# Layer 0 of a two-layer encoder: two modulation steps moved ahead, and the first gate's transpose put behind the keys' products

## The chip, the core and the metric

The kernel runs on one core of a Trainium2 chip. The metric is the time of one execution in microseconds (us), as the device gives it. Before the change three runs took 2202.97, 2203.79 and 2204.16 us; the median is 2203.79 us. Engines are named as in the profile: PE is TensorE (matrix products and transposes), DVE is VectorE, ACT is ScalarE, POOL is GpSimd, SP is the engine whose queue issues nearly all DMAs.

## What is computed

Two layers on x of 256 tokens by 2048 channels, conditioned on one vector c. The part that matters here:

```
c_act = silu(c)
for l in range(2):
    mod = c_act @ w_mod[l] + b_mod[l]            # 6 vectors of 2048
    shift_m, scale_m, gate_m, shift_f, scale_f, gate_f = split(mod, 6)
    h = layer_norm(x) * (1 + scale_m) + shift_m
    proj = h @ w_in[l]                            # four head groups A, B, C, D
    y = concat(A: gated MLP, B: latent attention, C: short conv, D: conformer conv) @ w_out[l]
    x = layer_norm(ALPHA * x + (1 + gate_m) * y) * g + b
    h = layer_norm(x) * (1 + scale_f) + shift_f
    x = layer_norm(ALPHA * x + (1 + gate_f) * conv_ffn(h)) * g + b
```

Group B squeezes h to latents, normalises them, turns them, and makes from them the rotated keys, the queries (`qn`, `qr`), the keys (`kn`) and the values (`vv`) for a four-head attention.

## The kernel before, in words

**Modulation as background work.** The 12 vectors of `mod` (six for each layer) are made on DVE. One vector is 16 steps; a step (`mod_block`, line 190) loads a block of `w_mod` of 128 x 2048 floats (1 MB) by SP's queue into one of four raw buffers and multiplies it with `crep` on DVE, with the sum over the columns as result (line 196). Layer 0's `SHIFT_M` and `SCALE_M` come first, in the planner of `by_blocks`. All other steps come from a generator, `mods`, in a fixed order that begins with `(0, GATE_M)` and goes on with `(0, SCALE_F)`.

**Pacing.** `stream` (line 337) treats one unit of weights: it loads the unit, records the products of the unit before, and calls `pump` (line 307). `pump` adds the rate of the present phase to a credit and takes one step for each whole credit. The rates stand in `RATES` (line 35); for layer 0 they are 1.3 a unit in phase B, 1.3 at each of four points inside the attention ("attend"), and 1.9 in phase C. Since the rows of a gate are needed across the partitions, `gate_rows` (line 268) turns the finished vector on PE (`turn`), copies it by ACT, writes it to DRAM (`line`) and reads it back to all partitions by SP (`spread`); both are chores that are tried after a step.

**The stretch around the change** (layer 0, some 150 to 330 us). Group B's latents are made from eight units of `w_in` of two pairs of 128 x 704 each (`latent_group`; the loads are named `wexact`), then four values' worth of weights for the attention are loaded (`wq`, `wkv`), then three steps are taken at once (`MODS_AHEAD`), and the latents are turned. Two DVE operations of the turned latents, `kc` and `kvr`, are tied behind the last of these three steps:

```
def behind(i):
    if stepped:
        tc.add_manual_dep(i.ins, stepped[0], order_dep, reason="these steps' weights land before the latents turn")
```

`kc` feeds the rotated key (`ps_kr` on PE). There are two PSUM buffers ("ms") for all these small products, so the first `ps_qn` needs the buffer that the second `kvr` reads. Meanwhile group C's eight units of products (`C_c`, 32 rows of the trace a unit) are recorded between the parts of the attention. DVE and ACT also work off, in the background, the 31 taps of group D's convolution (`convD`, `scaled`), and DVE the norm of group A's half (`va`), which needs a transfer `gmlp` into a raw buffer. Then comes the output projection: two units of plain float32 weights, then units whose weights ACT and DVE split into two parts (`whi` by ACT line 391, `wlo` by DVE line 400), and in between the rest of group D's norm: `ps_var`, `rd`, `dgD`, `ps_rD`.

Instructions are recorded in program order; a scheduler sets the order on each engine, and each engine then runs its list in order.

Of the kernel before, what the change touches and what calls it, by code (L numbers as in the profile page):

```python
# [31 lines left out]
SHIFT_M, SCALE_M, GATE_M, SHIFT_F, SCALE_F, GATE_F = range(6)  # L32


RATES = [
    dict(B=1.3, attend=1.3, C=1.9, out=1.0, out_next=0.0, out_last=0.0, out_tail=0.5, up_first=0.5, up_late=0.75, up_renewed=0.75, up_third=0.6, up=0.75, down=0.7, down_next=0.45, down_last=0.3, down_tail=0.5),
    dict(D=1.0, U=0.0, V=0.0, B=0.0, C=0.0, E=1.35, attend=0.0, out=0.75, out_next=0.6, out_last=0.0, out_tail=0.0, up_first=0.3, up_late=0.3, up_renewed=0.3, up_third=0.3, up=0.3, down=0.7, down_next=0.7, down_last=0.0, down_tail=0.0),
]

# [49 lines left out]
def encoder_kernel(ctx: ExitStack, tc: tile.TileContext, A: dict, consts: bass.AP, out: bass.AP):  # L89
# [22 lines left out]
    def ms_tile(name):  # L112
        return msp.tile([P, 512], F32, tag="ms", name=name)

    def acc_tile(name):
        return accp.tile([P, 512], F32, tag="acc", name=name)

    def mm(o, lhsT, rhs, start, stop):
        return pe.matmul(o, lhsT, rhs, start=start, stop=stop, skip_group_check=True)  # L119
# [4 lines left out]
    def slot(name, dtype=F32):  # L124
        return slotp.tile([P, 1024], dtype, tag="slot", name=name)
# [75 lines left out]

    GATE = {}
    closed = []
    GATES = [(l, m) for l in range(DEPTH) for m in (GATE_M, GATE_F)]

    chores = []
# [61 lines left out]
    def gate_rows(l, m, cols):  # L268

        line = dramp.tile([KT, P], F32, name=f"line_{l}_{m}")  # L270

        def turn():
            if pace["phase"].startswith("up"):
                return False
            ps = ms_tile("ps_gate")
            pe.transpose(ps[0:KT, 0:P], cols, ident)
            rows = keep.tile([KT, P], F32, tag="rows", name=f"rows_{l}_{m}")
            act.copy(rows, ps[0:KT, 0:P])
            nc.scalar.dma_start(out=line, in_=rows)
            return True  # L280

        def spread():
            if GATES.index((l, m)) > len(closed) + 1:
                return False
            if (l, m) == (1, GATE_M) and pace["phase"] in ("down", "down_next", "down_last", "down_tail", *"VDUBC"):
                return False
            g = gatep.tile([P, D], F32, tag="gate", name=f"gate_{l}_{m}")
            i = nc.sync.dma_start(out=g, in_=line.rearrange("k c -> (k c)").partition_broadcast(P))
            if (l, m) == (1, GATE_M):
                tc.add_manual_dep(i.ins, last_issue[0], order_dep, reason="layer 0's transfers come first")  # L290
            GATE[(l, m)] = g
            return True

        return [turn, spread]
# [3 lines left out]
        + [(0, GATE_F, 0, 3), late_steps, (0, GATE_F, 3, KT), (1, SHIFT_M), (1, SCALE_M)]  # L298
        + [(1, GATE_M), (1, SHIFT_F), (1, SCALE_F), (1, GATE_F)]
    )  # L300
    pace = {"rate": 0.0, "credit": 0.0, "phase": None}

    def phase(l, name):
        pace["phase"] = name
        pace["rate"] = RATES[l][name]

    def pump():
        pace["credit"] += pace["rate"]
        while pace["credit"] >= 1.0:
            pace["credit"] -= 1.0  # L310
            next(mods, None)
# [25 lines left out]
    def stream(load, products, bg=0):  # L337

        item = load()
        flush()  # L340
        pending.append(lambda: products(item))
        pump()
        for _ in range(min(bg, len(background))):
            background.pop(0)()
        if late["tasks"]:
            late["tasks"].pop(0)()
# [176 lines left out]
    def latent_group(w, c0, name, then, hF=None, bg=0):  # L523

        nk = 2
        box = {}

        def products(item, u):
            if u == 0:
                box["wide"] = [acc_tile(f"{name}_w{t}")[:, 0:Q_LORA] for t in range(2)]  # L530
                box["narrow"] = [acc_tile(f"{name}_n{t}")[:, 0 : 704 - Q_LORA] for t in range(2)]
                box["h"] = list(hT)
            for k, (hi, lo) in enumerate(item):
                kt = u * nk + k
                st, sp = kt == 0, kt == KT - 1
                for t in range(2):
                    tok = slice(t * P, (t + 1) * P)
                    outs = ((box["wide"][t], slice(0, Q_LORA)), (box["narrow"][t], slice(Q_LORA, 704)))
                    if lo is None:
                        for o, c in outs:  # L540
                            mm(o, hF(kt)[:, tok], hi[:, c], st, sp)
                        continue
                    xh, xl = (h[:, kt % 2, tok] for h in box["h"][kt // 2][:2])
                    for o, c in outs:
                        mm(o, xh, hi[:, c], st, False)
                    for o, c in outs:
                        mm(o, xh, lo[:, c], False, False)
                    for o, c in outs:
                        mm(o, xl, hi[:, c], False, sp)

        def load(u):
            return weights(w, u * nk, nk, c0, 704, hF is not None)

        return KT // nk, load, products, lambda: then(box["wide"], box["narrow"]), bg
# [27 lines left out]
    def run(g, ahead=0):  # L582
        units, load, products, end, bg = g
        loaded = []

        def get(u):
            while len(loaded) < min(u + 1 + (ahead if u > 0 else 0), units):
                loaded.append(load(len(loaded)))
            return loaded[u]

        for u in range(units):
            n = bg[u] if isinstance(bg, tuple) else bg
            stream(lambda: get(u), lambda item, u=u: products(item, u), n)
            pending.extend(postponed)
            postponed.clear()
        pending.append(end)
# [258 lines left out]
    def mixers(l, w_in, Y, hF=None, first_mod=None, quarter=None):  # L855
# [10 lines left out]
        def more_mods():  # L866
            pace["credit"] += RATES[l]["attend"]
            rate, pace["rate"] = pace["rate"], 0.0
            pump()
            pace["rate"] = rate  # L870
# [199 lines left out]
        def mix_b(wide, narrow):  # L1070
# [40 lines left out]


            steps = attend(WQ, WKV, lat, q01, rr)

            def step():
# [7 lines left out]
        def attend(WQ, WKV, lat, q01, rr):  # L1123
# [60 lines left out]
            for b in range(2):  # L1184
                ps = ms_tile("ps_kn")
                for hh in range(2):
                    h = 2 * b + hh
                    for j in range(2):
                        mm(
                            ps[:, hh * S : (hh + 1) * S],  # L1190
                            WKV[j][:, h * S : h * S + P],
                            kvr[:, j, :],
                            j == 0,
                            j == 1,
                        )
                act.copy(kn[:, 2 * b : 2 * b + 2, :], ps.rearrange("p (j s) -> p j s", j=2))
            more_mods()
            vv = slot("vv").rearrange("p (t c) -> p t c", t=2)
            for t in range(2):
# [143 lines left out]
        if hF is not None:  # L1343
            return by_blocks(l, w_in, hF, first_mod, quarter, mix_d, mix_u, gelu_v, mix_v, mix_b, mix_c, mix_e)
# [21 lines left out]
    def by_blocks(l, w_in, hF, first_mod, quarter, mix_d, mix_u, gelu_v, mix_v, mix_b, mix_c, mix_e):  # L1366
# [87 lines left out]
        sumE = total("E")  # L1454
        postponed.append(mix_v)
        phase(l, "B")
        run(latent_group(w_in, C_Q, f"B{l}", mix_b, hF=hf, bg=STEPS[l]["B"]))
        phase(l, "C")

# [329 lines left out]
def build(inputs):  # L1789
    import numpy as np  # L1790
    import concourse.bacc as bacc

    nc = bacc.Bacc("TRN2", target_bir_lowering=False, num_devices=1)
    v = {name: np.asarray(a, dtype=np.float32) for name, a in inputs.items()}
    arrays, A = {}, {}
    direct = {name: v[name] for name in _PLAIN}
    direct.update(params=_params(v), gmlp=_gmlp(v), consts=_constants(), late=_late(v))
    for name, a in direct.items():
        a = np.ascontiguousarray(a)
        arrays[f"in_{name}_dram"] = a  # L1800
        A[name] = nc.dram_tensor(f"in_{name}_dram", a.shape, F32, kind="ExternalInput").ap()
    for name in _PACKED:
        A[name] = Packed(nc, name, v[name].size)
    consts = A["consts"]
    out = nc.dram_tensor("out_0_dram", (1, S, D), F32, kind="ExternalOutput").ap()
    with tile.TileContext(nc) as tc:  # L1806
        encoder_kernel(tc, A, consts, out)
    for name in _PACKED:
        arrays[f"in_{name}_dram"] = A[name].array(v[name])
    return nc, arrays  # L1810
# [8 lines left out]
```

## Time and profile before

| | |
|---|---|
| median of three runs | 2203.79 us (2202.97 to 2204.16) |
| the profiled execution's own time | 2203.58 us |
| its span | 2201.8 us, so 1.8 us lie around it |
| PE busy | 2174.7 us, 99% of the span |
| DVE busy | 1740.8 us, 79% |
| ACT busy | 1101.8 us, 50% |
| DMA | 617.07 MB, mean 280 GB/s |

The profile is one execution. Busy times are sums over an engine's instructions; "idle before" is the time that an engine stood still in front of an instruction, with what ended it behind the arrow. [...]

### The profile page before, as it was taken

Reading aid. Unit: us, or ns where it says so; the run is one execution under the profiler, and the core shown is the slowest. Engines: PE = TensorE matmul, PEld = TensorE weight load, DVE = VectorE, ACT = ScalarE, POOL = GpSimd, SP = SyncE. Lnnn points to the kernel's source line nnn. Section 1 sums busy time; section 2 is a strip of 40 time slices with the busy share of each in tenths; the row PEclk is TensorE's granted clock in tenths of the full one; section 3 lists DMA queues with packets and bytes.
Section 4 is the critical chain, followed back from the end, with each engine's and each line's share of the span. In section 5 each row is a group of like instructions: output and inputs, shape, how many; then the busy total and the mean of one; then the engine's idle time right before and its main releaser. Section 6 shows DMA issues by size and latency. Waiting matters only on the chain. (4 is left out here: it accounts for less than half of the span.)

```text
span 2201.8 us, 28483 instructions
## 1 busy us (share of the span) xinstructions
PE 2174.7 (99%) x10916; PEld 1805.2 (82%) x10916; DVE 1740.8 (79%) x2325; ACT 1101.8 (50%) x1686; POOL 22.1 (1%) x40
## 2 busy tenths in 40 slices
PE   8999999999999999999999999999999999999997
PEld 6776878688888888888868988868888888888886
DVE  5658999789898888889978988977776755565777
ACT  3132744655555455545574545465444544454553
POOL 0000000000000000000000000000000000000000
PEclk9999999999999999999999999999999999999999
DMA  9999888688989988987768547956766655555554
GB/s 392 417 374 390 355 331 334 232 334 319 333 329 334 338 324 328 361 323 285 291 230 323 205 152 292 332 222 244 267 244 244 227 191 189 191 210 192 197 196 141
DMA packets 94906, 617.07 MB, mean 280 GB/s; under 512 B 10737, under 2 KB 10929, under 8 KB 27441
## 3 DMA queue, kind: packets, MB, share of 16 engines
q1 hardware_dynamic: 94466, 614.70, 75.2%
q8 instruction: 85, 1.39, 0.2%
q0 software_dynamic: 176, 0.53, 0.1%
q14 instruction: 51, 0.42, 0.0%
q10 hardware_dynamic: 128, 0.03, 0.0%
HBM read 613.08 MB, written 2.13 MB: 279 GB/s over the span
## 5 line engine op out<-in xcount | busy, mean ns | idle before, releaser
L391 ACT CAST whi<-wraw 128x1024 fp32r<-128x1024 f32 (+1 forms) x620 | 643.9, 1045 | 687.8 <-PE g_c L119 207.2
L400 DVE TENSOR_TENSOR wlo<-wraw,whi 128x1024 fp32r<-128x1024 f32 (+1 forms) x620 | 743.7, 1212 | 287.5 <-ACT whi L391 268.6
L119 PE MATMUL v_c<-hT,whi 128*128 128x512 f32 x1408 | 489.4, 392 | 0.0
L196 DVE SCALAR_TENSOR_TENSOR wmod<-wmod,crep 128x2048 f32<-128x2048 f32 x192 | 438.2, 2285 | 52.4 <-DMA wmod<-in_w_mod_dram 51.7
L119 PE MATMUL g_c<-hT,whi 128*128 128x512 f32 x1280 | 444.7, 392 | 0.0
L119 PE MATMUL v_c<-hT,wlo 128*128 128x256 f32 x1408 | 392.3, 279 | 0.0
L119 PE MATMUL d<-whi,a 128*128 128x512 f32 x1344 | 386.4, 389 | 0.0
L119 PE MATMUL g_c<-hT,wlo 128*128 128x256 f32 x1280 | 356.5, 278 | 0.0
L119 PEld LDWEIGHTS v_c<-hT,whi 128*128 128x128 f32 x1408 | 263.7, 187 | 59.4
L119 PEld LDWEIGHTS d<-whi,a 128*128 128x128 f32 x1344 | 252.0, 188 | 52.5
L119 PEld LDWEIGHTS g_c<-hT,whi 128*128 128x128 f32 x1280 | 239.7, 187 | 54.2
L119 PEld LDWEIGHTS v_c<-hT,wlo 128*128 128x128 f32 x1408 | 265.1, 188 | 0.0
L119 PEld LDWEIGHTS g_c<-hT,wlo 128*128 128x128 f32 x1280 | 241.0, 188 | 0.0
L119 PE MATMUL d<-wlo,a 128*128 128x512 f32 x672 | 232.9, 389 | 0.0
L119 PEld LDWEIGHTS d<-wlo,a 128*128 128x128 f32 x672 | 126.1, 188 | 26.2
L119 PE MATMUL o<-whi,a 128*128 128x512 f32 x416 | 121.4, 393 | 0.0
L119 PEld LDWEIGHTS o<-whi,a 128*128 128x128 f32 x416 | 78.6, 189 | 16.3
L425 DVE TENSOR_TENSOR a<-g,a 128x512 fp32r<-128x512 f32 x132 | 87.5, 682 | 0.0
L569 PE MATMUL first<-wexact,hN 128*128 128x512 f32 x192 | 85.5, 596 | 0.3
L421 ACT CAST a<-g 128x512 fp32r<-128x512 f32 x132 | 77.0, 615 | 0.0
L1535 DVE SCALAR_TENSOR_TENSOR u<-g,par,u 128x254 f32<-128x254 f32 (+1 forms) x176 | 74.3, 478 | 0.2
L119 PE MATMUL o<-wlo,a 128*128 128x512 f32 x208 | 72.8, 394 | 1.2 <-DVE wlo L400 1.2
(316 smaller groups left out, 2151.3 us busy)
## 6 DMA issues: line engine op xcount, KB each, us to landing
wmod<-in_w_mod_dram SPq DMA_DIRECT2D x192, 1024.0 KB, 7.2
wraw<-in_ffn_w_up_dram SPq DMA_DIRECT2D x168, 1024.0 KB, 5.2
wraw<-in_ffn_w_down_dram SPq DMA_DIRECT2D x88, 1024.0 KB, 5.1
wexact<-in_w_in_dram SPq DMA_DIRECT2D x64, 512.0 KB, 11.3
wraw<-in_w_out_dram SPq DMA_DIRECT2D x30, 1024.0 KB, 7.1
wraw<-in_w_in_dram SPq DMA_DIRECT2D x24, 1024.0 KB, 5.6
wexact<-in_ffn_w_up_dram SPq DMA_DIRECT2D x16, 512.0 KB, 5.0
wlate<-in_late_dram SPq DMA_DIRECT2D x8, 1024.0 KB, 6.5
```

The source lines that it names most:

```text
L119: return pe.matmul(o, lhsT, rhs, start=start, stop=stop, skip_group_check=True)
L196: i = dve.scalar_tensor_tensor(out=raw, in0=raw, scalar=1.0, in1=crep, op0=ALU.mult, op1=ALU.mult, accum_out=col)
L391: i = act.copy(hi[:, :m], r)
L400: i = dve.tensor_tensor(out=lo[:, :m], in0=r, in1=hi[:, :m].bitcast(F32), op=ALU.subtract)
L421: i = act.copy(hi, src)
L425: dve.tensor_tensor(out=lo, in0=src, in1=hi.bitcast(F32), op=ALU.subtract)
L569: i = pe.matmul(ps, hN[kt // 4][:, kt % 4, t * P : (t + 1) * P], parts[kt], start=kt == 0, stop=kt == KT - 1, skip_group_check=True,)
L1535: dve.scalar_tensor_tensor(out=u[:, sh:], in0=x[:, : S - sh], scalar=col(k, j), in1=u[:, sh:], op0=ALU.mult, op1=ALU.add)
```

## The change

Three things. In phase C the rate falls from 1.9 to 1.65 a unit. In phase B the first three units each get 0.7 of credit on top of 1.3 (`pace["more"]`); so two steps more are taken in group B's units and two fewer in group C's. And `turn` of `(0, GATE_M)` refuses until `keyed` holds something, which is so once the keys' products (`ps_kn`) have been recorded.

```diff
-    dict(B=1.3, attend=1.3, C=1.9, out=1.0, ...
+    dict(B=1.3, attend=1.3, C=1.65, out=1.0, ...
...
     closed = []
+    keyed = []
...
         def turn():
             if pace["phase"].startswith("up"):
                 return False
+            if (l, m) == (0, GATE_M) and not keyed:
+                return False
             ps = ms_tile("ps_gate")
             pe.transpose(ps[0:KT, 0:P], cols, ident)
...
-    pace = {"rate": 0.0, "credit": 0.0, "phase": None}
+    pace = {"rate": 0.0, "credit": 0.0, "phase": None, "more": []}
...
     def pump():
         pace["credit"] += pace["rate"]
+        if pace["more"]:
+            pace["credit"] += pace["more"].pop(0)
...
                 act.copy(kn[:, 2 * b : 2 * b + 2, :], ps.rearrange("p (j s) -> p j s", j=2))
+            keyed.append(True)
             more_mods()
...
         phase(l, "B")
+        pace["more"] = [0.7, 0.7, 0.7]
         run(latent_group(w_in, C_Q, f"B{l}", mix_b, hF=hf, bg=STEPS[l]["B"]))
```

What this does to the engines' lists shows at three places. In the changed kernel line numbers behind line 204 are up to seven higher.

The first is SP's queue through group B's units. `wexact` 128x704 is a unit's pair of weights, `wmod` a step's block. Before:

```order
L375 DMA wexact<-in_w_in_dram 128x704 x2
L194 DMA wmod<-in_w_mod_dram 128x2048
L375 DMA wexact<-in_w_in_dram 128x704 x2
L1033 DMA gmlp<-in_gmlp_dram 128x2048
L194 DMA wmod<-in_w_mod_dram 128x2048
L375 DMA wexact<-in_w_in_dram 128x704 x2
L194 DMA wmod<-in_w_mod_dram 128x2048
L375 DMA wexact<-in_w_in_dram 128x704 x2
L194 DMA wmod<-in_w_mod_dram 128x2048 x2
```

With the change:

```order
L380 DMA wexact<-in_w_in_dram 128x704 x2
L194 DMA wmod<-in_w_mod_dram 128x2048 x2
L380 DMA wexact<-in_w_in_dram 128x704 x2
L1038 DMA gmlp<-in_gmlp_dram 128x2048
L194 DMA wmod<-in_w_mod_dram 128x2048 x2
L380 DMA wexact<-in_w_in_dram 128x704 x2
L194 DMA wmod<-in_w_mod_dram 128x2048 x2
L380 DMA wexact<-in_w_in_dram 128x704 x2
L194 DMA wmod<-in_w_mod_dram 128x2048
```

Six blocks instead of three stand ahead of the fourth unit's pair, one fewer stands behind it, and ten becomes twelve over the eight units; the three blocks of `MODS_AHEAD` stay where they are, behind `wkv`, and are now the 13th to 15th instead of the 11th to 13th.

The second is DVE from the first steps of `(0, GATE_M)` to the turned latents' `kc`. The rows from the first step on, before:

```order
L196 SCALAR_TENSOR_TENSOR wmod,sums_2_837<-wmod,crep 128x2048
L1038 BN_STATS stA<-va 128x6 x2
L603 BN_AGGR mv_A_867<-stA 128x2
L603 BN_AGGR mv_A_876<-stA 128x2
L605 TENSOR_SCALAR rs_A_869<-mv_A_867 128x1
L605 TENSOR_SCALAR rs_A_878<-mv_A_876 128x1
L1421 TENSOR_TENSOR partE<-E_0_811,partE 128x512
L938 TENSOR_TENSOR convD<-convD,scaled 128x4x255
L1421 TENSOR_TENSOR partE<-E_1_812,partE 128x512
```

With the change:

```order
L196 SCALAR_TENSOR_TENSOR wmod,sums_2_837<-wmod,crep 128x2048
L1043 BN_STATS stA<-va 128x6 x2
L196 SCALAR_TENSOR_TENSOR wmod,sums_2_837<-wmod,crep 128x2048
L1427 TENSOR_TENSOR partE<-E_0_811,partE 128x512
L1427 TENSOR_TENSOR partE<-E_1_812,partE 128x512
L608 BN_AGGR mv_A_870<-stA 128x2
L608 BN_AGGR mv_A_879<-stA 128x2
L943 TENSOR_TENSOR convD<-convD,scaled 128x4x255
L610 TENSOR_SCALAR rs_A_872<-mv_A_870 128x1
L610 TENSOR_SCALAR rs_A_881<-mv_A_879 128x1
```

The second step has moved from behind the four `va` operations to ahead of `partE`; behind the rows shown one more tap (128x4x254), then the four `va` operations and then the third step follow. Later on, eight steps in a row stand ahead of `kc` before, and nine with the change; the third of `MODS_AHEAD` is the last of them in both.

The third is PE at the output projection's first split unit (`o_...`; `ps_var` and `ps_rD` belong to group D's norm). Before:

```order
L119 MATMUL ps_var<-ones,sqD_1680 128x1 x2
L119 MATMUL ps_var<-ones,sqD_1681 128x1 x2
L119 MATMUL o_000_1655<-whi,a 128x512
L119 MATMUL o_001_1656<-whi,a 128x512
L119 MATMUL o_000_1655<-wlo,a 128x512
```

With the change:

```order
L119 MATMUL ps_var<-ones,sqD_1680 128x1 x2
L119 MATMUL ps_var<-ones,sqD_1681 128x1 x2
L119 MATMUL ps_rD<-dgD,ones 128x256
L119 MATMUL o_000_1655<-whi,a 128x512
L119 MATMUL o_001_1656<-whi,a 128x512
L119 MATMUL o_010_1657<-whi,a 128x512
L119 MATMUL o_011_1658<-whi,a 128x512
L119 MATMUL o_000_1655<-wlo,a 128x512
```

`ps_rD` stood 28 products further on and now comes directly behind `ps_var`. Elsewhere on PE, `ps_gate` moves from among group C's products to behind `ps_kn`, the first transpose of the latents moves from ahead of group C's first unit to behind it, and most of group C's second and third unit moves from ahead of `ps_qr` and `ps_kn` to behind the scores.

## Rows read from the trace of the kernel before

**Rows 1.** The page, busy time of PE: us, share of span, instructions.

```profile
PE 2174.7 (99%) x10916; PEld 1805.2 (82%) x10916; DVE 1740.8 (79%) x2325; ACT 1101.8 (50%) x1686; POOL 22.1 (1%) x40
```

**Rows 2.** Waits of PE, first 450 us: us in total, times, longest.

```profile
...
PE ps_qn L119 <- DVE kvr L1151: 1.2, 1, 1.2
PE o L119 <- DVE wlo L400: 1.2, 2, 0.9
PE ps_kr L119 <- DVE kc L1147: 1.2, 1, 1.2
PE o L119 <- DMA wexact<-in_w_out_dram: 1.1, 1, 1.1
...
```

**Rows 3.** Busy time by stretch, last three columns: PE's clock, DMA share, GB/s.

```profile
core 0: us, PE busy (x) PEld busy (x) DVE busy (x) ACT busy (x) POOL busy (x), PEclk, DMA share, GB/s
...
160.00:172.00 12.00, 12.00 (x55) 8.80 (x54) 10.74 (x15) 7.41 (x19) 0.11 (x1) 1.00 0.65 234
172.00:210.00 38.00, 37.04 (x137) 25.23 (x135) 28.41 (x27) 8.04 (x26) 1.63 (x3) 1.00 1.02 416
...
232.00:240.00 8.00, 8.00 (x38) 6.79 (x38) 8.00 (x10) 6.98 (x19) 0.00 (x0) 1.00 0.18 51
240.00:290.00 50.00, 49.90 (x240) 42.24 (x240) 49.73 (x70) 28.07 (x71) 0.00 (x0) 1.00 0.93 370
```

**Rows 4.** Timeline of SP's queue: start us, us, what, how many.

```profile
162.54 6.36 SPq L194 DMA_DIRECT2D wmod<-in_w_mod_dram  x2
168.98 0.86 SPq L375 DMA_DIRECT2D wexact<-in_w_in_dram  x2
```

**Rows 5.** Timeline of DVE: start us, us, what, how many, idle before.

```profile
164.92 1.41 DVE L1043 SCALAR_TENSOR_TENSOR va<-va,rs_A,gmlp 128x512 f32<-128x512 f32 x2
166.25 2.28 DVE L196 SCALAR_TENSOR_TENSOR wmod<-wmod,crep 128x2048 f32<-128x2048 f32 x1
...
207.65 2.29 DVE L196 SCALAR_TENSOR_TENSOR wmod<-wmod,crep 128x2048 f32<-128x2048 f32 x1 [0.19 <-DMA wmod<-in_w_mod_dram]
...
210.13 2.29 DVE L196 SCALAR_TENSOR_TENSOR wmod<-wmod,crep 128x2048 f32<-128x2048 f32 x1 [0.17 <-DMA wmod<-in_w_mod_dram]
...
212.34 0.41 DVE L1146 TENSOR_TENSOR kc<-ps_q,cst 64x256 f32<-64x256 f32 x1
...
215.61 0.47 DVE L1151 TENSOR_SCALAR kvr<-ps_kv,par 128x256 f32<-128x256 f32 x1
```

**Rows 6.** Timeline of PE, the turned latents and what follows.

```profile
202.87 7.07 PE L119 MATMUL C_c<-hF,wexact 128*128 128x256 f32 x32
...
213.23 0.67 PE L119 MATMUL ps_kr<-kc,cst 64*128 64x256 f32 x2 [1.18 <-DVE kc L1147]
...
216.14 8.30 PE L119 MATMUL ps_qn<-qg,wq 128*128 128x256 f32 x24 [1.24 <-DVE kvr L1151]
224.28 11.39 PE L119 MATMUL C_c<-hF,wexact 128*128 128x256 f32 x52
```

**Rows 7.** Busy time by stretch, columns as in rows 3: where the clock was low.

```profile
215.00:222.00 7.00, 5.86 (x14) 4.71 (x15) 4.39 (x6) 3.86 (x10) 0.00 (x0) 0.51 1.04 415
...
314.00:318.00 4.00, 4.00 (x12) 3.10 (x12) 3.12 (x7) 3.27 (x3) 0.70 (x1) 0.57 0.99 412
```

**Rows 8.** Timeline of PE at the output projection's start.

```profile
295.88 14.00 PE L119 MATMUL o<-wexact,ya 128*128 128x512 f32 x32 [1.13 <-DMA wexact<-in_w_out_dram]
309.71 1.84 PE L119 MATMUL ps_var<-ones,sqD 128*128 128x1 f32 x16
...
313.04 0.73 PE L119 MATMUL o<-wlo,a 128*128 128x512 f32 x2 [0.91 <-DVE wlo L400]
```

**Rows 9.** Timeline of DVE, group D's deviation.

```profile
316.24 0.15 DVE L985 TENSOR_SCALAR rd<-ps_var 128x2 f32<-128x2 f32 x1
317.28 0.48 DVE L991 TENSOR_SCALAR dgD<-cst,rd 128x128 f32<-128x128 f32 x2 [0.88 <-POOL rd L149]
```

More of the change, by code (lines that the diff above doesn't have):

```diff
@@ L35 @@
 RATES = [
-    dict(B=1.3, attend=1.3, C=1.9, out=1.0, out_next=0.0, out_last=0.0, out_tail=0.5, up_first=0.5, up_late=0.75, up_renewed=0.75, up_third=0.6, up=0.75, down=0.7, down_next=0.45, down_last=0.3, down_tail=0.5),
+    dict(B=1.3, attend=1.3, C=1.65, out=1.0, out_next=0.0, out_last=0.0, out_tail=0.5, up_first=0.5, up_late=0.75, up_renewed=0.75, up_third=0.6, up=0.75, down=0.7, down_next=0.45, down_last=0.3, down_tail=0.5),
     dict(D=1.0, U=0.0, V=0.0, B=0.0, C=0.0, E=1.35, attend=0.0, out=0.75, out_next=0.6, out_last=0.0, out_tail=0.0, up_first=0.3, up_late=0.3, up_renewed=0.3, up_third=0.3, up=0.3, down=0.7, down_next=0.7, down_last=0.0, down_tail=0.0),
```

## The prediction

> **What bounds the kernel now.** I read the page first: PE is busy for 2174.7 of 2201.8 us [rows 1], so the end moves only by what PE loses or wins: waits, and products at the lower clock. Next the waits of PE in the first 450 us, the only part that the change reorders to any extent: two waits of 1.2 us in the turned latents (for `kc` and for `kvr`), 1.1 us for the first weights of the output projection, and two for `wlo`, 0.9 and 0.3 us [rows 2]. The timeline shows where they lie [rows 6, 8]. The clock's stretches show what comes on top: PE had half of its clock around 215 to 222 us and again around 314 to 318 us [rows 7], each time just behind such waits. The 24 products of `ps_qn` took 8.30 us; at full clock a product of this size takes 0.22 us (32 `C_c` in 7.07 us), which makes 5.3 us, so the first low stretch cost 3.0 us [rows 6]. The second cost about half of 0.43 x 2 x 4.0 us = 1.7 us [rows 7]. All that can be won here is thus near 2.4 + 3.0 + 1.1 + 1.2 + 1.7 = 9.4 us, 0.4% of the time. I count a move under 0.2%, or 4.4 us, as no change, about what a measurement can tell.
>
> **What sets the start of `ps_qn`.** The timeline of DVE answers it: `kc` starts at 212.34, right behind the third of the steps of MODS_AHEAD, and that step (and the one before it) had waited for its block; the two landed 2.48 us apart [rows 5]. So the keys' chain hangs on the 13th block of the first gate, not on DVE. And the queue that brings it was full: from 172 to 210 us the share is 1.02 at 416 GB/s, while from 160 to 172 it was 0.65 [rows 3].
>
> **Part 1, two steps into group B's units.** They put two more blocks of 2.48 us ahead of the block that `kc` hangs on. Used as it is now, the queue brings it 5.0 us later. Could the empty time before 172 us take them in? There are 12 x 0.35 = 4.2 us of it [rows 3], which would leave 0.8 us. But a block needs one of four raw buffers. The second one of the row at 162.54 shows that: its issue took place at 162.54 + 6.36 - 0.33 = 168.57 us, when the second step's product, started at 166.25, had freed a buffer [rows 4, 5]. With the change the sixth block waits in the same way for the third step's product, and that stands behind the `va` operations. These ended at 166.3 us [rows 5]; the new order puts a tap, and four small operations, behind `partE` that were done before it or came later, some 1.2 + 0.6 us, so they end near 168.0, the third product near 170.3, and the sixth block is issued 1.8 us later than the fifth is now. Behind it the fourth unit's pair is still to come (2 x 352 KB, 1.7 us at 416 GB/s), which now goes ahead, and nine blocks instead of eight. By that count the 15th block is 1.8 + 1.7 + 2.5 = 6.0 us late. I take 5.5 us, between 5.0 and 6.0, since both rest on the same full queue; 0.8 stays as the lower bound. The second `kvr` stands one step behind `kc` in both orders, so `ps_qn` starts 5.5 us later. That the first transpose of the latents no longer waits ahead of group C's first unit gives nothing: PE would only wait longer for `kc`. The pairs of group B's units come later too, by a few us; no wait of PE for them stands in rows 2, and a delay of them is covered by the wait for `kc`, which is 7 us or so long now.
>
> **The clock.** In the trace PE was at its lower level for some 5.9 us after `ps_qn` had started (216.14 to 222) and, in the other stretch, for about 4.5 us after the wait that ended at 313.04 [rows 6, 7, 8]. With a longer wait more of the low stretch lies in the wait itself. Ends: nothing at the lower clock (3.0 us won), or all 24 products (10.6 us, 2.3 us lost). I take 1.0 us won, a little beyond what the second stretch's 4.5 us would give (0.7 us). [...] The trace shows the low level behind both gaps (0.51 and 0.57).
>
> **Part 2, two steps fewer in group C, and the gate's transpose.** DVE was busy 49.73 of 50 us from 240 to 290 [rows 3], so two products of 2.29 us fewer let it reach the projection at worst 5.5 - 4.6 = 0.9 us later, while PE comes 5.5 - 1.0 = 4.5 us later. Hence PE's wait of 1.1 us for `wexact` of the output projection goes: its issues follow DVE's steps. The longest waits of PE hold none for group C's products [rows 2]; I cost the new order of group C's products at nothing, since three `C_c` rows of the order, six products or 1.3 us, stand between `ps_qr` and each `ps_qr2` and cover `qc`; without that cover two waits of up to 1.3 us come. The gate's transpose no longer stands among these products; its DMA chain still blocks SP until `line` has landed (share 0.18 from 232 to 240 [rows 3]), now about 3 us later. No wait followed from it before, and the units of group C have been loaded in advance; I cost it at nothing.
>
> **Part 3, `ps_rD`.** It is now directly behind `ps_var`, and must wait for `rd` (0.15), POOL (0.88) and `dgD` (0.48) [rows 9]: 1.6 us with the hops, in which PE does nothing. In turn the wait for `wlo` of 0.9 us is covered, and with it I count the 0.3 us of rows 2: +0.4. The second low stretch I leave as it is, for a wait of this kind stands there again.
>
> **The sum:** + 5.5 - 1.0 - 1.1 + 0.4 = + 3.8 us. The profiled execution took 2203.58 us (2201.8 and 1.8 around it), 0.2 under the median of 2203.79; on that median the forecast is **2207.6 us**, which is 0.17% more, no change by the bound, if close to it.
>
> **Rivals.**
> A, the queue takes the blocks in: the 15th block is 0.8 us late. For it speaks the share of 0.65; against it the buffers. Then 0.8 - 1.0 - 1.1 + 0.4 = - 0.9, and with shorter waits both low stretches may go, 2.0 and 1.7 more: down to - 4.6, 2199.2 us.
> B, slower: the clock stays low through `ps_qn`. Its place is the 24 products behind the long wait, its price 2.3 us lost where I have 1.0 won, so + 7.1, 2210.9 us. It decides if the low stretch still lasts 7 us after `ps_qn` has started; for it speaks that PE will have stood nearly still for longer than in any row, against it that both stretches ended within 5.9 us of PE's restart. [...]
> C, the lateness is made up: DVE, two steps ahead, spares PE every later wait and the 1.6 us too, and the second low stretch goes: 3.8 - 1.6 - 1.7 = + 0.5, about 2204.3 us. That the change does nothing else than it says is not in doubt: the lists of all engines are those of the order.
>
> **How the numbers follow.** Forecast 0.53, with its own range of 2205.5 to 2209.5; of it 0.38 lies within 0.2% and 0.15 beyond. A 0.17, of which 0.10 is faster by over 0.2% and 0.07 within. B 0.20, all slower. C 0.10, within. So faster 0.10, within 0.2% 0.55, slower 0.35. The range leaves out half of A and the upper half of B: 2200 to 2211.5 us. It takes in the bounds of the clock, of the covers (2 x 1.3) and of the queue.
>
> **What would show it.** DVE's `kc` should start near 217.8 instead of 212.34, behind a step that waited for its block; PE's wait for `kc` should be near 7 us; `ps_qn` should start near 221.6 and take 6.5 to 8 us. The wait for `wexact` at the projection should be gone, and a wait of 1.6 us for `dgD` should stand there. If `kc` starts before 214, part 1 is wrong; if `ps_qn` takes 10 us, B is right; if no wait for `dgD` shows, part 3 is.

## The result and the profile after

The changed kernel took 2207.49 us (median of 14 runs, 2205.78 to 2209.94), the kernel before 2202.49 us (14 runs on the same chip, 2201.56 to 2204.62): a ratio of 1.0022, 95% interval 1.0015 to 1.0029. It is slower by some 5 us; that is little, but the two ranges don't overlap. The profiled execution of the change was its shortest (2205.78 us, span 2204.0), that of before (2203.58) was 1.1 us above its median; so the two traces differ by 2.2 us where the medians differ by 5.0. A second trace of the change, from the experiments, shows what the first one hides.

DVE at the turned latents, the rows that answer to those of [rows 5]:

```profile
210.76 2.29 DVE L196 SCALAR_TENSOR_TENSOR wmod<-wmod,crep 128x2048 f32<-128x2048 f32 x1 [8.23 <-DMA wmod<-in_w_mod_dram]
...
215.73 2.29 DVE L196 SCALAR_TENSOR_TENSOR wmod<-wmod,crep 128x2048 f32<-128x2048 f32 x1 [0.18 <-DMA wmod<-in_w_mod_dram]
...
217.95 0.41 DVE L1151 TENSOR_TENSOR kc<-ps_q,cst 64x256 f32<-64x256 f32 x1
...
221.21 0.47 DVE L1156 TENSOR_SCALAR kvr<-ps_kv,par 128x256 f32<-128x256 f32 x1
```

`kc` stands behind the 15th product now, and that one behind its block; it starts at 217.95 instead of 212.34, 5.6 us later. PE's timeline there and at the projection (the counterparts of [rows 6, 8]):

```profile
210.49 0.44 PE L1139 MATMUL ps_kv<-cst,lat 128*128 128x128 f32 x2 [0.23 <-ACT qg L1145]
218.83 1.19 PE L119 MATMUL ps_kr<-kc,cst 64*128 64x256 f32 x2 [7.91 <-DVE kc L1152]
...
221.74 6.70 PE L119 MATMUL ps_qn<-qg,wq 128*128 128x256 f32 x24
...
298.17 13.90 PE L119 MATMUL o<-wexact,ya 128*128 128x512 f32 x32
311.90 1.84 PE L119 MATMUL ps_var<-ones,sqD 128*128 128x1 f32 x16
315.36 0.70 PE L119 MATMUL ps_rD<-dgD,ones 128*128 128x256 f32 x2 [1.62 <-DVE dgD L996]
```

One wait of 7.9 us has taken the place of the two of 1.2; no wait for `wexact` stands at the projection; `ps_rD` waits 1.62 us for `dgD`. Of the waits of PE in the first 450 us (the counterpart of [rows 2]), these three lie in the part that was changed:

```profile
PE ps_kr L119 <- DVE kc L1152: 7.9, 1, 7.9
...
PE ps_rD L119 <- DVE dgD L996: 1.6, 1, 1.6
...
PE o L119 <- DVE wlo L405: 0.2, 1, 0.2
```

The busy time by stretch, with PE's clock, DMA share and GB/s last (the counterpart of [rows 3, 7]; the first two stretches are those of the low clock, 0.50, where the third has the full one, 1.00):

```profile
214.10:224.30 10.20, 5.47 (x12) 3.40 (x13) 9.70 (x13) 2.44 (x7) 0.00 (x0) 0.50 1.01 410
316.50:319.90 3.40, 3.40 (x10) 2.63 (x9) 3.40 (x4) 0.00 (x0) 0.00 (x0) 0.50 0.38 92
160.00:172.00 12.00, 12.00 (x54) 8.83 (x53) 11.09 (x22) 8.80 (x23) 2.55 (x3) 1.00 0.51 193
```

The queue between 160 and 172 us is emptier than before (0.51 against 0.65) although it had more to bring. SP's timeline says why (the counterpart of [rows 4]), with DVE's third step:

```profile
160.37 10.06 SPq L194 DMA_DIRECT2D wmod<-in_w_mod_dram  x2
```

```profile
167.78 2.29 DVE L196 SCALAR_TENSOR_TENSOR wmod<-wmod,crep 128x2048 f32<-128x2048 f32 x1
```

The second of these two issues took place at 160.37 + 10.06 - 0.33 = 170.10 us (0.33 us is what one such issue takes without a wait, as that at 156.86 us): it had to wait for a buffer until the third step's product, which stands behind the `va` operations, had ended at 170.07.

To compare executions whole, I use the lag of PE: the start of one product less the start of group B's first product, against the trace of before (161.92 us there). The points are the starts of the first and the last product of `ps_qn`, of the first of the projection, and of the transposes of layer 0's and layer 1's second norms (before: 216.14, 224.06, 295.88, 391.94 and 1451.64 us). In us, minus is earlier:

| trace | ps_qn first | ps_qn last | projection | norm, layer 0 | norm, layer 1 |
|---|---|---|---|---|---|
| the change | +5.8 | +4.2 | +2.5 | +2.8 | +2.1 |
| the change, second trace | +4.9 | +4.7 | +3.0 | +4.6 | +3.6 |
| e1 kc behind the 13th step | -0.1 | -1.2 | -1.7 | -1.3 | -2.3 |
| e2 before, kc behind the 11th | -0.8 | -3.7 | +3.7 | +6.2 | +5.3 |
| e3 pacing without the gate's delay | +10.5 | +7.5 | +3.4 | +2.2 | +1.3 |
| e4 the gate's delay alone | -0.1 | -0.7 | -0.4 | -1.1 | -1.8 |
| e6 that, and two steps fewer in C | -0.4 | -0.6 | -2.3 | -0.8 | -2.2 |
| e7 kc behind the 11th, gate late | -0.8 | -2.2 | +0.6 | +1.2 | +0.2 |
| e9 the change, rd behind wlo | +4.9 | +4.8 | +3.0 | +2.4 | +1.5 |
| e10 the change, kc freed, gate late | -3.0 | -5.9 | -1.6 | -2.5 | -3.5 |
| e11 kc freed, old pacing, gate late | -1.8 | -4.7 | +5.1 | +3.5 | +3.1 |
| e12 e10 once more | -3.0 | -4.2 | -1.0 | -2.2 | -3.2 |

In some executions, of more than one kernel, the time is longer by several us (e1: 2210.02 and 2211.20 us beside ten runs from 2201.54 to 2204.85), with the products of a long stretch of the FFN 2% slower in the trace of e1; the profiled executions of e8 and e11, 4.7 and 5.7 us above their medians, are taken to be of this kind, so the spans of these three are not used, and their lags only up to that stretch (e8 has no row).

### The profile page after: what moved, and what is told of

Its sections match the earlier page's. It is cut to its first block, busy times and chain, and to the rows that moved or that the text cites. A ratio compares the mean times of both kernels' runs of the same rounds, so it can differ in the third digit from the quotient of the medians.

```text
span 2204.0 us, 28478 instructions
## 1 busy us (share of the span) xinstructions
PE 2173.4 (99%) x10916; PEld 1809.8 (82%) x10916; DVE 1741.5 (79%) x2325; ACT 1100.5 (50%) x1686; POOL 23.3 (1%) x40
```

## The experiments

Each was compared with the kernel before on its own chip. The ratio is to that kernel; its median was 2202.33 us for e1 to e4, 2202.01 for e5 to e8, 2202.03 for e9 and e10, 2204.11 for e11 and e12. The ratio is an estimate with its interval and not the quotient of the two medians; the two differ most where the times scatter (e11: 1.0015 and 1.0026).

### The chain: which block kc hangs on (e1, e2, e3)

**e1**, the change with `kc` and `kvr` tied to the first of the three steps of MODS_AHEAD (the 13th) instead of the third (the 15th):

```diff
                 for _ in range(MODS_AHEAD):
                     next(mods, None)
-                stepped.append(last_step[0])
+                    stepped.append(last_step[0])
```

> The changed kernel, with one edit: kc and kvr are tied behind the first of the three steps of MODS_AHEAD instead of the third; number and places of all steps stay. Theory (the start of ps_qn hangs on the last block that kc is tied to): the 13th block's product ran 210.76 to 213.05 us in the changed kernel, so kc starts near 213.1 instead of 217.95, the second kvr stands behind the 14th product (213.25 to 215.5) and starts near 215.6, ps_qn starts near 216.2 as before the change, PE's wait for kc falls from 7.9 to about 3 us with 1.5 us for kvr, and the time falls by about 4 us to 2203.5 us, the kernel before within 1 us. Rival (kc is late because the latents' transposes moved behind group C's first unit on PE): kc stays behind 216 us, ps_qn near 221, the time stays at 2207.5 us.

Measured: 2202.8 us, ratio 1.0000 (0.9988 to 1.0013). The loss is gone by this one order, within the interval. `kc` started as soon as the 13th product ended:

```profile
209.66 2.29 DVE L196 SCALAR_TENSOR_TENSOR wmod<-wmod,crep 128x2048 f32<-128x2048 f32 x1 [8.24 <-DMA wmod<-in_w_mod_dram]
211.88 0.08 DVE L196 DVE_READ_ACCUMULATOR wmod<-wmod,crep 128x1 f32 x1
211.88 0.41 DVE L1151 TENSOR_TENSOR kc<-ps_q,cst 64x256 f32<-64x256 f32 x1
```

PE waited 2.29 us for it and none for `kvr`, less than was expected, in part since the 13th block had landed 1.1 us earlier than in the change (209.66 against 210.76); `ps_qn` started at 215.67 us. The rival falls: the latents' transposes stand behind group C's first unit here as in the change.

**e2**, the same edit in the kernel before.

> The kernel before, with the same single edit: kc tied behind the 11th step instead of the 13th. In the list of DVE the second kvr now stands behind the 12th product alone. Theory (the block sets kc): the 11th block had landed at 205.07 us, so kc is bound by PE's transposes instead and starts near 211.5; the first kvr follows, then the 12th product of 2.3 us, then the second kvr near 214.5, so ps_qn starts 1.0 us earlier than 216.14; PE's two waits of 1.2 us shrink to about 1.4 in all. Gain 1 us, and up to 4 us if the low stretch of the clock behind them goes too: 2198.5 to 2201.5 us. Rival (DVE and PE, not the block, set kc in the kernel before): kc stays at 212.3, the time within 1 us of the kernel before.

Measured: 2210.75 us, ratio 1.0038 (1.0023 to 1.0052). Neither said this. The chain did what the theory says (`kc` at 211.30, second `kvr` at 214.58, `ps_qn` at 215.10 us, and, with 5.45 us for its 24 products, at full clock), but the win of 3.7 us was lost at once:

```profile
215.10 5.45 PE L119 MATMUL ps_qn<-qg,wq 128*128 128x256 f32 x24 [1.24 <-DVE kvr L1151]
220.39 14.84 PE L119 MATMUL C_c<-hF,wexact 128*128 128x256 f32 x68
239.00 0.27 PE L276 MATMUL ps_gate<-cst,mod 128*16 128x128 f32 x1 [3.77 <-DVE mod L229]
```

In the list of PE the gate's transpose stands ahead of the queries' `ps_qr`, as before, but on DVE the 16th step now comes behind eight taps (225.45 us, 10.05 us for the eight). So PE waits for the gate, and with it the whole attention; waits of 1.6 us for the softmax's `p`, 1.6 for `wexact` and 2.6 for `wlo` follow, and the products right behind the gate's are slow: four `C_c` take 1.91 us there, where four ahead of the latents' transposes took 1.03.

**e3**, the pacing of the change without the gate's delay:

```diff
...
-            if (l, m) == (0, GATE_M) and not keyed:
-                return False
...
```

> The change without its third part: two steps more in group B's units, two fewer in group C's, but the gate's transpose may go as soon as its vector is done. It then stands ahead of the latents' transposes on PE, and needs the sum behind the 16th step. Theory (PE works its list in order, and the blocks set the steps): the 16th block landed at 218.14 us in the changed kernel, its product takes 2.29 us, so ps_gate starts near 220.7 with a wait of about 12 us of PE behind group C's first unit, the latents turn only then, kc starts near 222.5 and ps_qn near 225: some 3.5 us behind the changed kernel, 2211 us. Rival (the keys' products hide it, so this part is worth nothing): within 1 us of the changed kernel's 2207.5 us.

Measured: 2209.69 us, ratio 1.0028 (1.0013 to 1.0042), with runs from 2204.83 to 2215.52. `ps_gate` waited 11.56 us, to 219.89, and with it the latents' transposes, which stand behind it in PE's list and follow at 220.05 us; `ps_qn` came 10.5 us late in lag:

```profile
219.89 0.37 PE L276 MATMUL ps_gate<-cst,mod 128*16 128x128 f32 x1 [11.56 <-DVE mod L229]
```

So the third part spares PE 3.7 us of waiting here. What that is worth in time isn't shown: the interval takes in the change's 1.0022. At the layer's second norm this trace lags by only 2.2 us, less than the change: behind its one long wait no wait above 0.25 us is left up to 420 us, and the clock is at 1.00 from 290 to 330 us. But it is the trace of e3's shortest run, 4.9 us under the median; why the median is then as high as the change's stays open.

### The third part alone (e4), and with two steps fewer (e6)

**e4** keeps `keyed` and has the old pacing:

```diff
-    dict(B=1.3, attend=1.3, C=1.65, out=1.0, ...
+    dict(B=1.3, attend=1.3, C=1.9, out=1.0, ...
...
-        pace["more"] = [0.7, 0.7, 0.7]
```

> The third part alone: the steps are those of the kernel before, but the gate's transpose waits until the keys' products are recorded. Theory (this part costs and gains nothing by itself): kc, kvr and ps_qn stay at 212.3, 215.6 and 216.1 us within 0.3; the order of group C's products behind ps_qn changes and SP's wait for the gate's line ends some 3 us later; the time stays within 1.5 us of the kernel before. Rival (part of the 5 us comes from here, by SP standing behind the line or by group C's products): the time is 2 us or more above the kernel before.

Measured: 2201.83 us, ratio 1.0002 (0.9992 to 1.0013); `kc` 212.51, second `kvr` 215.77, `ps_qn` 216.30 us. The part by itself costs nothing. PE's wait for `wexact` grew to 1.79 us.

**e6** is e4 with C = 1.65 again; of e4's edit only the second part is left.

> The third part of the change with two steps fewer in group C's units, and none more in group B's. Theory (what costs is the two steps ahead of kc; the two fewer behind it gain the wait for wexact at the projection): kc at 212.5 and ps_qn at 216.3 us as in the kernel before, the wait for wexact, 1.8 us with the third part alone, falls under 0.5, the second waits as there; 1 to 1.5 us below the kernel before, 2201 us. Rival (DVE's lateness in group C doesn't set the projection): the wait for wexact stays over 1.5 us, no gain.

Measured: 2209.83 us, ratio 1.0037 (1.0024 to 1.0050): a miss, but an instructive one. At the projection it is right: no wait for `wexact`, 1.9 us ahead of e4 in lag. Then the win goes in two places. `ps_rD` moves to directly behind `ps_var` here too and waits 1.62 us, so that at the next norm e6 is 0.3 us behind e4. And over 1,100 us later the two steps are missed, since nothing has taken them in. These are PE's waits between 1400 and 1500 us, of which the kernel before has only the second, at 0.2:

```profile
PE first L574 <- ACT hN L122: 6.3, 1, 6.3
PE ps_xT L631 <- ACT xn L122: 0.3, 1, 0.3
```

ACT's `hN` waited 6.49 us for DVE's `mod` of layer 1's second half, and PE's clock was low for part of the time behind it (0.66 from 1452 to 1462 us). So the steps are one budget with a due date in layer 1: group C may have two fewer only because group B has two more.

### The clock: a second trace of the change (e5)

**e5** has no edit: it is the changed kernel once more.

> The changed kernel unchanged, for a second trace: its profiled execution (span 2204.0 us, mean clock 0.995) was the shortest of its 14, 1.7 us under their median, and its lag behind the trace of before was only 2.2 us at the end where the medians differ by 5.0 us. Theory (the rest of the difference is clock: PE's low stretch behind the long wait for kc lasts longer in most executions): the waits of PE repeat within 0.3 us (7.9 for kc, 1.6 for dgD), kc starts at 217.9 again, and where the span is longer, ps_qn takes more than 6.7 us or a third low stretch shows, 2 us of low clock for each us of span. Rival (the rest lies elsewhere, in no part of the change): the lag at the end of ps_qn is 4.0 to 4.2 us again, at the second norm of layer 0 (the transposes near 394 us) 2.7 again, and what is longer comes after that.

Measured: 2206.36 us, ratio 1.0021 (1.0009 to 1.0033), the same loss again; the profiled execution took 2207.06 us. The wait for `dgD` repeats (1.61 us); that for `kc` is 0.6 us shorter, 7.28 us, where 0.3 was allowed, and `kc` starts at 216.90, 1.0 earlier. The low clock doesn't repeat:

```profile
217.79 1.19 PE L119 MATMUL ps_kr<-kc,cst 64*128 64x256 f32 x2 [7.28 <-DVE kc L1152]
...
220.69 8.11 PE L119 MATMUL ps_qn<-qg,wq 128*128 128x256 f32 x24
```

And by stretch:

```profile
212.50:226.10 13.60, 8.31 (x19) 5.62 (x20) 11.44 (x14) 3.58 (x9) 0.00 (x0) 0.50 1.02 414
314.90:321.70 6.80, 6.01 (x14) 4.76 (x15) 6.29 (x10) 1.22 (x2) 0.22 (x1) 0.50 0.46 164
```

The first low stretch lasted 13.6 us instead of 10.2, the second 6.8 instead of 3.4. `ps_qn` took 1.4 us more, and the lag grows by 1.6 us between the projection and the norm where the first trace has 0.4. What this trace loses beyond the first comes from these two places. So the rival falls, and the theory holds as to the place; that the waits repeat within 0.3 us does not.

### ps_rD (e9)

**e9** ties `rd` behind the `wlo` of the first split unit:

```diff
-                dve.tensor_scalar(
+                i = dve.tensor_scalar(
...
+                if hF is not None and last_low[0]:
+                    tc.add_manual_dep(i.ins, last_low[0], order_dep, reason="the first split unit goes first")
```

> The changed kernel with one more order: rd on DVE stands behind the wlo of the first split unit, so that ps_rD on PE goes 48 products further on, and PE needn't wait for dgD. Theory (part 3's new place of ps_rD costs its wait and the low clock behind it: the lag grew by 0.4 us over this stretch in one trace of the change and by 1.6 in the other, where the third part alone won 0.7): the wait of 1.6 us for dgD goes, wlo is ready in time, the low stretch near 316 us goes or shrinks, and the time falls by 1.5 to 3 us, to 2203.5 to 2205 us. Rival (the wait only moves, to wlo or to the products of group D's half): a wait of 1 us or more for another releaser stands between 312 and 345 us, and the time stays within 0.7 us of the changed kernel.

Measured: 2205.78 us, ratio 1.0013 (1.0004 to 1.0022). Its trace has the lag of e5 up to the projection (4.8 at the end of `ps_qn`, 3.0), and then:

```profile
310.00:330.00 20.00, 19.27 (x88) 15.05 (x87) 15.24 (x17) 7.29 (x8) 0.70 (x1) 1.00 0.77 283
```

The wait for `dgD` and the second low stretch are gone. In their place stand waits of 0.72, 0.33 and 0.93 us for `wlo` at 327, 336 and 350 us, so the wait moves in part, as the rival has it; still, of the 4.6 us of e5 at the norm 2.4 are left. So 2.2 us lie between these two traces. By the times it is 0.6: e9 is 3.8 us above the kernel before, e5 was 4.4, and the intervals overlap. The traces exaggerate it, as the profiled execution of e9 was 0.9 us under its median and that of e5 0.7 above. As to the time the rival is thus right (within 0.7 us of the change); that the place of `ps_rD` costs the time that the theory gave it is not shown.

### A reserve: what is won ahead of group C (e7, e8, e10, e11, e12)

**e7** is e2 with the gate's transpose held back until the first scores; **e8** is e7 with C = 1.65. The test of `keyed` is that of the change; against the change, the place where it is filled moves:

```diff
-            keyed.append(True)
             more_mods()
...
             p1 = softmax(1, 0)
+            keyed.append(True)
```

> The kernel before with kc tied behind the 11th step, as in the earlier run that had a wait of 3.8 us for the gate's vector, but with the gate's transpose held back until the first scores are recorded, so that this wait can't stand ahead of the queries. Steps as in the kernel before. Theory of a reserve (what PE wins ahead of group C it gives back at the projection, since DVE is busy through group C and its steps set wexact): kc near 211.3, ps_qn from 215.1 to 220.2 us, 3.7 us earlier than before, and then PE's wait for wexact grows from 1.1 to between 3 and 5 us; the time is within 1.5 us of the kernel before. Rival (the win stays): the wait for wexact stays under 2 us, the time falls by 3 us or more, under 2199.5 us.

Measured: 2204.48 us, ratio 1.0008 (0.9999 to 1.0016). The win is given back at the projection, as the theory says, and a little more is lost there (the time itself, 2.5 us above the kernel before by medians, is not clear of noise):

```profile
296.29 15.70 PE L119 MATMUL o<-wexact,ya 128*128 128x512 f32 x32 [3.48 <-DMA wexact<-in_w_out_dram]
```

PE waits 3.48 us for `wexact`, and the 32 products behind it take 15.70 us instead of 14.00 [rows 8], 1.70 us more. By my estimate that is 3.4 us at a clock of 0.50; the traces of e12 and e11 have this clock at the same place, from 295.5 to 298.9 and from 298.3 to 305.0 us.

> The same, with two steps fewer in group C's units (4.6 us of DVE's products less ahead of the projection). Theory of a reserve: now the win of 3.7 us stays, and the wait for wexact is under 1.5 us: 2198 to 2199.5 us, faster than both kernels. Rival (the win is lost elsewhere, by a wait for the gate, the softmax or wlo): the time is over 2201 us with a wait of 2 us or more of PE between 225 and 320 us.

Measured: 2210.95 us, ratio 1.0037 (1.0024 to 1.0050). The wait for `wexact` was 0.42 us as expected, but two more were not: `ps_qn` took 8.45 us behind the same waits as in e7, and the missing steps cost a wait of 6.1 us for `hN` in layer 1, as in e6. So its time tells nothing on the reserve. Up to layer 0's second norm its trace does: it is 1.3 us ahead of before there, where e7 is 1.2 us behind.

**e10** has the change's pacing, takes the three steps behind the turned latents, and holds the gate as e7 does:

```diff
-                for _ in range(MODS_AHEAD):
-                    next(mods, None)
-                stepped.append(last_step[0])
+                stepped.append(None)
...
+            if stepped:
+                after_turn[0] = turned_last[0]
+                for _ in range(MODS_AHEAD):
+                    next(mods, None)
+                after_turn[0] = None
```

(`turned_last` is the second `kvr`; `mod_block` ties a step behind `after_turn`; `behind` no longer ties `kc`.)

> The change's pacing (two steps more in group B, two fewer in C), but the three steps of MODS_AHEAD come behind the turned latents (order only), so that kc and kvr wait for no block of theirs, and the gate's transpose waits for the first scores. Theory of a reserve (PE's waits from 200 to 320 us stand for one another; what sets the projection is DVE in group C and the weights whose issue follows it): kc near 210.5, ps_qn starts near 214 us, 2 us ahead of the kernel before, its low stretch shrinks, and PE gives it back in a wait for wexact of 2 to 3.5 us; the time is within 1 us of the kernel before. Rival (with two products fewer in group C the win stays): the wait for wexact is under 1 us, the time 2199.5 us or less, faster than both.

Measured: 2200.26 us, ratio 0.9991 (0.9982 to 1.0000). The time lies between the two: `ps_qn` started 3.0 us earlier than before in lag and at full clock (1.00 from 210 to 225 us), and of this lead, 5.9 us at its last product, 2.5 us are left at the norm. In between PE waited 2.01 us for `pT` and 1.79 for `wexact` (before: 1.13), and lost some 1.7 us in a low stretch of the clock behind the first of these, 0.50 from 258.4 to 261.8 us.

```profile
212.65 5.45 PE L119 MATMUL ps_qn<-qg,wq 128*128 128x256 f32 x24 [0.46 <-ACT rope L1170]
```

**e11** is e10 with the old pacing (the edit of e4), **e12** is e10 again beside it.

> As the run with the three steps behind the turned latents, but with the pacing of the kernel before (ten steps in group B's units, 1.9 a unit in group C). It asks whether the change's pacing is worth anything once no block holds kc. Theory (it is: two products of 2.29 us fewer on DVE between the turned latents and the projection are what lets PE keep the win): kc near 211 and ps_qn from 213 us as there, low clock in ps_qn gone too, but PE's wait for wexact is longer by 2.5 to 4.6 us than the 1.8 us there, and the time is 2.5 to 4.5 us above that run, 2203 to 2205 us. Rival (only the tie matters): the wait for wexact is 2 us or less, the time within 1 us of that run, 2199.5 to 2201.5 us.

> The run with the change's pacing and the three steps behind the turned latents once more, beside the other pacing on one chip, for the interval: it had 2200.26 us against 2202.03, 0.9991 (0.9982 to 1.0). Theory: again 1 to 2.5 us below the kernel before, ps_qn at its full clock (5.4 us), a wait for wexact of 1.5 to 2.5 us and one of 2 us for pT. Rival (the first was a lucky chip): within 0.5 us of the kernel before.

Measured: e11 2209.79 us, ratio 1.0015 (0.9996 to 1.0035), runs from 2204.95 to 2217.19; e12 2200.82 us, ratio 0.9986 (0.9968 to 1.0005). The traces separate them: at the projection e11 lags by 5.1 us and e12 is 1.0 ahead. In e11:

```profile
300.80 16.10 PE L119 MATMUL o<-wexact,ya 128*128 128x512 f32 x32 [4.16 <-DMA wexact<-in_w_out_dram]
```

A wait of 4.16 us for `wexact` (2.58 in e12) and one of 1.20 for a pair of group C. So the theory holds in the traces: once no block holds `kc`, the two steps moved from group C to group B are worth some 6 us there, more than was expected. By the times it isn't settled, since the two intervals overlap. In e12 itself one thing failed: `ps_qn` was not at full clock, it took 7.08 us. Against the kernel before, each on its own chip, e10 and e12 are 1.8 and 3.3 us ahead by medians, where the change was 4.4 to 5.0 behind; in the traces' last column both are over 3 us ahead. Both intervals lie below those of the change (1.0015 and e5's 1.0009 at their lower ends), but against the kernel before each ends at or just above 1.

## Why the prediction came out so

The predicted time was 2207.6 us, the measured median 2207.49. That is closer than the reasoning deserves: the sum was + 3.8 us on a base of 2203.79, while the larger sample puts the base at 2202.49 and the difference at 5.0 (4.4 in e5's comparison). The likeliest case, no change by over 0.2%, was just missed on its slow side: 1.0022. Term by term, first and second trace:

- **Keys' chain, + 5.5: right.** + 5.8 and + 4.9, and `kc` at 217.95 where 217.8 was named. e1 shows the cause: tie `kc` to the 13th block, and it is gone. The buffers' part of the working holds, too: the sixth block issued at 170.10, 1.5 us later than the fifth before (1.8 were counted).
- **Clock, - 1.0: the term that was mis-sized, as a single number.** `ps_qn` took 6.70 and 8.11 us against 8.30, so - 1.6 and - 0.2. My reason was that a longer wait takes more of the low stretch into itself. It did: 1.0 us of it lay in the wait before (215.1 to 216.14), 4.7 and 5.3 in the two traces (214.1 to 218.83, 212.5 to 217.79). But the stretch itself was longer, too, 10.2 and 13.6 us instead of 6.8. Before, the low clock lasted 5.9 us beyond the start of `ps_qn` (the second stretch, which I read as 4.5 us, had 3.4 us of low clock by its own row, 0.57 over 4 us [rows 7]); now it lasted 2.6 us in one trace (221.74 to 224.3) and 5.4 in the other (220.69 to 226.1). So a gain followed in the first and hardly any in the second, and one number for it claimed more than could be known. Rival B needed 7 us there, which neither trace reached.
- **Wait for `wexact`, - 1.1: right.** It is gone, and e4 and e6, which differ in group C's rate alone, show by what: 1.79 us with the old rate, none with two steps fewer. Between the last product of `ps_qn` and the projection both traces win 1.7 us, 0.6 more than that wait, for which I have no row.
- **`ps_rD`, + 0.4: the wait right, the sum right for one trace alone.** The wait was 1.62 us as worked out, and `wlo`'s waits fell from 1.2 to 0.2 us. But "the second low stretch I leave as it is" held for the first trace (3.4 us) and not for the second (6.8): between the projection and the norm they lose 0.4 and 1.6 us, and e9, the change without the wait, had no low stretch there.
- **Not in the sum:** 0.7 to 0.9 us are won back between the two norms, where the kernel before waits 0.8 us for `sqD` (at 1358 us) and neither trace of the change does.

The terms as measured give + 2.1 and + 3.6 at layer 1's norm, a mean of 2.9 against the 3.8 predicted. The rest of the medians' difference is the place of the profiled executions beside their medians. That of before, on which all lags rest, was 1.1 us above its median (1.6 above that of e5's chip); the change's was 1.7 us under, e5's 0.7 above. So 2.1 + 1.1 + 1.7 = 4.9 us answers to the 5.0 measured, and 3.6 + 1.6 - 0.7 = 4.5 to e5's 4.4. Which stretch of the trace of before was longer I could not settle.

Rival A (the queue takes the blocks in) fell by `kc`. Rival C (the lateness is made up) fell in its numbers, but its mechanism is at work: the trace of e3, with twice the delay, had a smaller lag at the norm than either trace of the change (2.2 us against 2.8 and 4.6), though it is that of e3's shortest run.

## What to carry to other kernels

A small operation that is tied behind a prefetched block inherits that block's place in a full queue (here a DMA share of 1.02 [rows 3], two blocks more, and `kc` 5.6 us later): before adding transfers ahead, ask which consumers are tied to the last of them, and move the tie with them. With the tie moved two steps forward the loss was gone (e1); with no tie the pacing was worth some 6 us in the traces (e12 against e11). As made, the tie turned it into a loss. And moving background work out of one stage is only free if another takes it: a fixed budget of steps showed its due date over 1,100 us later (in e6, a wait of 6.3 us).

## What the runs showed of the hardware

The low stretch of PE's clock was not fixed by the program here. e2, e7 and e8 have the same two waits ahead of `ps_qn` (0.34 and 1.24 us), and its 24 products took 5.45, 6.91 and 8.45 us; e10 and e12 are one kernel, have the same waits within 0.01 us, none above 0.47 in the 10 us ahead of `ps_qn`, and had 5.45 and 7.08:

```profile
215.02 8.45 PE L119 MATMUL ps_qn<-qg,wq 128*128 128x256 f32 x24 [1.24 <-DVE kvr L1156]
```

```profile
213.64 7.08 PE L119 MATMUL ps_qn<-qg,wq 128*128 128x256 f32 x24 [0.47 <-ACT rope L1170]
```

The first row is e8's, the second e12's. The wait of 1.24 us thus cost nothing more in e2, and 3 us more in e8. e10 and e12 ran on two chips, but e7 and e8 on one, so the chip alone doesn't decide it; what does stays open. I had taken such a stretch as a repeatable term.

The FFN's products didn't run equally fast at the same granted clock: from 1500 to 1950 us PE was busy all the time and the clock at 1.00 in both of these rows, the first of before, the second of e1, but it did 2598 products in one and 2549 in the other, 2% fewer. The products with `whi` took 399 ns each in e1 against 394, those with `wlo` 281 against 277. I saw no cause for it in the kernel.

```profile
1500.00:1950.00 450.00, 450.00 (x2598) 393.34 (x2596) 299.71 (x395) 229.81 (x327) 0.00 (x0) 1.00 0.63 221
```

```profile
1500.00:1950.00 450.00, 450.00 (x2549) 390.12 (x2549) 293.99 (x387) 224.38 (x320) 0.00 (x0) 1.00 0.62 216
```
